# Row 6 subtracted in parts, the last row cut into other pieces, and a first transfer issued by a second engine, in a row-wise sum of |x - y|

## The chip, the cores and the metric

One core of a Trainium2 chip. The metric is device time in microseconds (us). The granted clock is 1.00. The profiled span is some 1.8 us shorter than the time of the same execution (span 86.1 for a time of 87.86), because it leaves out what surrounds the program.

## The reference

```python
def setup_inputs():
    batch, dim = 1024, 4096
    return {"x": np.random.randn(batch, dim).astype(np.float32),
            "y": np.random.randn(batch, dim).astype(np.float32), "axis": -1}

def reference(x, y, axis):
    return np.sum(np.abs(x - y), axis=axis).astype(np.float32)
```

Both inputs are 16.8 MB, so 33.55 MB must come in, and 4 KB go out. With 128 partitions each partition holds 8 rows of 4096 columns, called rows 0 to 7 here.

## The kernel before

VectorE (DVE) subtracts, ScalarE (ACT) takes the absolute value and sums it through its accumulator: each ACTIVATE is followed by an ACTIVATION_READ_ACCUMULATOR that writes the sum out, called the read below. Rows 0 to 3 of x and of y come in one transfer each. Rows 4 to 6 of x come next; their y rows go into the buffer that the first four y rows leave, one transfer as each is used up. Row 7 comes in four pieces, x and y each. The last of the pieces is subtracted and then summed by DVE itself, together with ACT's sums of the others.

```python
PIECES = [2304, 1152, 512, 128]
# ... (K = 8 rows a partition, H = 4, n_part = 3; tiles xa, xb, yb: [128, H, 4096], ro: [128, K])
        nc.sync.dma_start(out=xa, in_=xr[:, 0:H, :])
        nc.sync.dma_start(out=yb, in_=yr[:, 0:H, :])
        nc.sync.dma_start(out=xb[:, 0:H - 1, :], in_=xr[:, H:K - 1, :])

        def whole(tx, ty, k):
            nc.vector.tensor_sub(out=tx, in0=tx, in1=ty)
            nc.scalar.activation(tx, tx, ABS, accum_out=ro[:, k:k + 1])
# ... (rows 0 to 3: whole(); after each, y's row 4, 5, 6 or row 7's x and y pieces are issued)
        for k in range(H - 1):
            whole(xb[:, k, :], yb[:, k, :], H + k)
        tx, ty = xb[:, H - 1, :], yb[:, H - 1, :]
        o = 0
        for i, w in enumerate(PIECES):
            s = slice(o, o + w)
            if i < n_part:
                nc.vector.tensor_sub(out=tx[:, s], in0=tx[:, s], in1=ty[:, s])
                nc.scalar.activation(tx[:, s], tx[:, s], ABS, accum_out=last[:, i:i + 1])
            else:
                nc.vector.tensor_sub(out=last[:, n_part:n_part + w], in0=tx[:, s], in1=ty[:, s])
                nc.vector.reduce_sum(out=ro[:, K - 1:K], in_=last, axis=AX, apply_absolute_value=True)
            o += w
        nc.sync.dma_start(out=orr, in_=ro)
```

Of the kernel before, what the change touches and what calls it, by code (L numbers as in the profile page):

```python
# [5 lines left out]

F32 = mybir.dt.float32
ABS = mybir.ActivationFunctionType.Abs
AX = mybir.AxisListType.X

PIECES = [2304, 1152, 512, 128]


@with_exitstack
def kernel(ctx, tc, x, y, axis, out):
    nc = tc.nc
    P = nc.NUM_PARTITIONS
    R, C = x.shape
    K = R // P
    xr = x.rearrange("(p k) c -> p k c", p=P, k=K)  # L20
    yr = y.rearrange("(p k) c -> p k c", p=P, k=K)
    orr = out.rearrange("(p k) -> p k", p=P, k=K)
    assert sum(PIECES) == C
    n_part = len(PIECES) - 1
    H = K // 2
    ps = ctx.enter_context(tc.tile_pool(name="ps", bufs=1))
    with tc.manual_schedule():
        xa = ps.tile([P, H, C], F32, tag="xa")
        xb = ps.tile([P, H, C], F32, tag="xb")

        yb = ps.tile([P, H, C], F32, tag="yb")
        ro = ps.tile([P, K], F32, tag="ro")

        last = ps.tile([P, n_part + PIECES[-1]], F32, tag="last")
        nc.sync.dma_start(out=xa, in_=xr[:, 0:H, :])  # L35
        nc.sync.dma_start(out=yb, in_=yr[:, 0:H, :])
        nc.sync.dma_start(out=xb[:, 0:H - 1, :], in_=xr[:, H:K - 1, :])

        def whole(tx, ty, k):
            nc.vector.tensor_sub(out=tx, in0=tx, in1=ty)  # L40
            nc.scalar.activation(tx, tx, ABS, accum_out=ro[:, k:k + 1])  # L41

        for k in range(H):
            whole(xa[:, k, :], yb[:, k, :], k)
            if k < H - 1:
                nc.sync.dma_start(out=yb[:, k, :], in_=yr[:, H + k, :])
                continue
            o = 0
            for w in PIECES:
                nc.sync.dma_start(out=xb[:, k, o:o + w], in_=xr[:, K - 1, o:o + w])  # L50
                nc.sync.dma_start(out=yb[:, k, o:o + w], in_=yr[:, K - 1, o:o + w])
                o += w
        for k in range(H - 1):
            whole(xb[:, k, :], yb[:, k, :], H + k)
        tx, ty = xb[:, H - 1, :], yb[:, H - 1, :]
        o = 0
        for i, w in enumerate(PIECES):
            s = slice(o, o + w)
            if i < n_part:
                nc.vector.tensor_sub(out=tx[:, s], in0=tx[:, s], in1=ty[:, s])  # L60
                nc.scalar.activation(tx[:, s], tx[:, s], ABS, accum_out=last[:, i:i + 1])  # L61
# [7 lines that stand above are left out]
# [1 line left out]
_INS = ['x', 'y', 'axis']  # L70
_OUTS = [((1024,), 'float32')]

_NUMBERS = {'axis': -1}


# [26 lines left out]
```

## Time and profile before

| | before |
|---|---|
| time, median of 4 runs | 87.82 us (87.72 to 87.96) |
| profiled span | 86.1 us |
| data coming in | from about 1.7 to 81.4 us, without a rest |
| last reduce ends | 83.77 us |

The busy row of the page (engine, busy us, share of the span, instructions) and the DMA queue (packets, MB, share of 16 engines' span):

```profile
DVE 35.8 (42%) x12; ACT 31.2 (36%) x21; POOL 0.2 (0%) x4
...
q1 hardware_dynamic: 2160, 33.56, 92.0%
```

Neither engine is half busy, while the one DMA queue works for 92% of the span. This is how to read such a kernel: first the stream that carries the data, and its end; then what is left to do after the last byte.

### The profile page before, as it was taken

The page shows a single profiled execution, that of the slowest core. Times are in us where ns is not written, and L with a number is a line of the kernel's source. Part 1 is how long each engine was busy: PE and PEld are TensorE (multiplying, and loading weights), DVE is VectorE, ACT ScalarE, POOL GpSimd, SP SyncE. Part 2 cuts the span into 40 slices and gives each one's busy share as a digit, 9 for nine tenths or more (in the row PEclk, how much of TensorE's full clock was granted, in tenths as well). Part 3 has the DMA queues.
Part 4 walks back from the last instruction along what each step waited for, and adds up shares of the span by engine and source line. Part 5 has one row for each costly group of instructions (what it writes and reads, how often), then busy time and mean ns, then how long its engine had stood idle before and what let it go on. Part 6 is the DMA issues. An engine that isn't in the chain of part 4 may idle for free.

```text
span 86.1 us, 104 instructions
## 1 busy us (share of the span) xinstructions
DVE 35.8 (42%) x12; ACT 31.2 (36%) x21; POOL 0.2 (0%) x4
## 2 busy tenths in 40 slices
DVE  0000000000000000000499999996498989939920
ACT  0000000000410000000004979797933949589970
POOL 0000000000000000000000000000000000000000
DMA  9199999768999999777998889899999999999400
GB/s 426 61 487 487 487 487 487 335 274 365 487 487 487 487 487 487 335 305 335 502 594 365 365 365 457 365 434 442 411 449 411 442 402 411 428 398 401 152 0 2
DMA packets 2160, 33.56 MB, mean 390 GB/s; under 512 B 368, under 2 KB 624, under 8 KB 1136
## 3 DMA queue, kind: packets, MB, share of 16 engines
q1 hardware_dynamic: 2160, 33.56, 92.0%
HBM read 33.55 MB, written 0.00 MB: 390 GB/s over the span
## 4 chain that ended last, share of the span: by engine, by line
DMA 67%; DVE 24%; ACT 5%; SPq 0%; issue 0%; ACTq 0%; DVEq 0%
DMA yb<-in_y_dram 67%; DVE xa L40 20%; ACT xb L61 5%; DVE xb L60 3%; SPq L35 0%; DVE ro L64 0%; ACTq L97 0%; DVEq L60 0%; DVEq L40 0%
## 5 line engine op out<-in xcount | busy, mean ns | idle before, releaser
L40 DVE TENSOR_TENSOR xa<-xa,yb 128x4096 f32<-128x4096 f32 x4 | 17.4, 4420 | 42.0 <-DMA yb<-in_y_dram 42.0
L41 ACT ACTIVATE xa<-xa 128x4096 f32<-128x4096 f32 x4 | 14.5, 3616 | 24.4 <-DVE xa L40 24.4
L40 DVE TENSOR_TENSOR xb<-xb,yb 128x4096 f32<-128x4096 f32 x3 | 13.3, 4426 | 2.9 <-DMA yb<-in_y_dram 2.9
L41 ACT ACTIVATE xb<-xb 128x4096 f32<-128x4096 f32 x3 | 10.8, 3616 | 5.0 <-DVE xb L40 5.0
L41 ACT ACT_TABLE_LOAD x1 | 1.3, 1283 | 22.6 <-DMA xa<-in_x_dram 22.6
L60 DVE TENSOR_TENSOR xb<-xb,yb 128x2304 f32<-128x2304 f32 (+2 forms) x3 | 4.6, 1537 | 1.6 <-DMA yb<-in_y_dram 1.6
L61 ACT ACTIVATE xb<-xb 128x2304 f32<-128x2304 f32 (+2 forms) x3 | 3.9, 1294 | 0.1
L64 DVE TENSOR_REDUCE ro<-last 128x1 f32<-128x131 f32 x1 | 0.3, 290 | 1.5 <-ACT xb L61 1.5
L41 ACT ACTIVATION_READ_ACCUMULATOR xa<-xa 128x1 f32 x4 | 0.7, 186 | 0.0
L41 ACT ACTIVATION_READ_ACCUMULATOR xb<-xb 128x1 f32 x3 | 0.6, 186 | 0.0
L61 ACT ACTIVATION_READ_ACCUMULATOR xb<-xb 128x1 f32 x3 | 0.6, 186 | 0.0
L63 DVE TENSOR_TENSOR last<-xb,yb 128x128 f32<-128x128 f32 x1 | 0.3, 285 | 0.0
L83 POOL MEMSET const-bfloat16-1.0<- 128x1 bf16 x1 | 0.1, 102 | 0.0
L83 POOL MEMSET const-uint8-127<- 128x1 uint8 x1 | 0.1, 101 | 0.0
L83 POOL MEMSET const-float32-0.0<- 128x1 f32 x1 | 0.1, 99 | 0.2 <-issue 0.2
L83 POOL MEMSET const-float32-1.0<- 128x1 f32 x1 | 0.1, 98 | 0.0
## 6 DMA issues: line engine op xcount, KB each, us to landing
xb<-in_x_dram SPq DMA_DIRECT2D x1, 6144.0 KB, 54.8
yb<-in_y_dram SPq DMA_DIRECT2D x3, 2048.0 KB, 15.4
xb<-in_x_dram SPq DMA_DIRECT2D x1, 1152.0 KB, 18.5
yb<-in_y_dram SPq DMA_DIRECT2D x1, 1152.0 KB, 17.3
xb<-in_x_dram SPq DMA_DIRECT2D x1, 576.0 KB, 18.4
yb<-in_y_dram SPq DMA_DIRECT2D x1, 576.0 KB, 19.3
xb<-in_x_dram SPq DMA_DIRECT2D x1, 256.0 KB, 19.5
yb<-in_y_dram SPq DMA_DIRECT2D x1, 256.0 KB, 19.7
```

What stands on the lines that cost most here:

```text
L40: nc.vector.tensor_sub(out=tx, in0=tx, in1=ty)
L41: nc.scalar.activation(tx, tx, ABS, accum_out=ro[:, k:k + 1])
L60: nc.vector.tensor_sub(out=tx[:, s], in0=tx[:, s], in1=ty[:, s])
L61: nc.scalar.activation(tx[:, s], tx[:, s], ABS, accum_out=last[:, i:i + 1])
L63: nc.vector.tensor_sub(out=last[:, n_part:n_part + w], in0=tx[:, s], in1=ty[:, s])
L64: nc.vector.reduce_sum(out=ro[:, K - 1:K], in_=last, axis=AX, apply_absolute_value=True)
L83: nc = _bacc.Bacc("TRN2", target_bir_lowering=False, num_devices=1)
```

## The change

It cuts row 6 into three subtractions and three ACTIVATEs so that ACT may begin before the whole row is subtracted. It makes row 7's pieces more even. It lets ACT issue the first y transfer while SP (SyncE) issues the first x transfer.

```diff
-PIECES = [2304, 1152, 512, 128]
+PIECES = [1984, 1088, 640, 384]
+ROW6 = [2048, 1024, 1024]
@@
+        part6 = ps.tile([P, n6], F32, tag="part6")
@@
-        nc.sync.dma_start(out=yb, in_=yr[:, 0:H, :])
+        nc.scalar.dma_start(out=yb, in_=yr[:, 0:H, :])
@@
-        for k in range(H - 1):
+        for k in range(H - 2):
             whole(xb[:, k, :], yb[:, k, :], H + k)
+        o = 0
+        for i, w in enumerate(ROW6):
+            tx, ty = xb[:, H - 2, o:o + w], yb[:, H - 2, o:o + w]
+            nc.vector.tensor_sub(out=tx, in0=tx, in1=ty)
+            nc.scalar.activation(tx, tx, ABS, accum_out=part6[:, i:i + 1])
+            o += w
@@ in the loop over PIECES
+            if i == 1:
+                nc.vector.reduce_sum(out=ro[:, K - 2:K - 1], in_=part6, axis=AX)
```

More of the change, by code (lines that the diff above doesn't have):

```diff
@@ L24 @@
     n_part = len(PIECES) - 1
+    n6 = len(ROW6)
     H = K // 2
```

## The prediction

> **What bounds the kernel now**
>
> The page's DMA rows and the stretches come first, because 33.55 MB must come in and the engines are busy only 42% and 36% of the span. In the stretches, columns are from:to, length, busy time of each engine, clock, DMA busy share and GB/s:
>
> ```profile
> 4.30:15.00 10.70, 0.00 (x0) 0.00 (x0) 0.00 (x0) 1.00 1.13 490
> ...
> 60.00:76.80 16.80, 13.28 (x3) 11.78 (x7) 0.00 (x0) 1.00 1.00 422
> ```
>
> A share above 1 is an artefact: a packet counts where it starts. What is to be seen is that the DMA engines do not rest from the first packet to the last. The list of DMA issues, with the time from issue to landing, gives the landings:
>
> ```profile
> xb<-in_x_dram SPq DMA_DIRECT2D x1, 1152.0 KB, 18.5
> yb<-in_y_dram SPq DMA_DIRECT2D x1, 1152.0 KB, 17.3
> xb<-in_x_dram SPq DMA_DIRECT2D x1, 576.0 KB, 18.4
> yb<-in_y_dram SPq DMA_DIRECT2D x1, 576.0 KB, 19.3
> xb<-in_x_dram SPq DMA_DIRECT2D x1, 256.0 KB, 19.5
> yb<-in_y_dram SPq DMA_DIRECT2D x1, 256.0 KB, 19.7
> ...
> yb<-in_y_dram SPq DMA_DIRECT2D x1, 64.0 KB, 10.3
> xa<-in_x_dram SPq DMA_DIRECT2D x1, 21.8
> yb<-in_y_dram SPq DMA_DIRECT2D x1, 40.7
> ```
>
> Issue times from the timeline (0.73 for xa, 1.16 for the first y, then 55.49, 59.45, 59.82, 60.30, 60.79, 61.35 and 71.14) plus these give: xa lands at 22.5, the first y at 41.9, x2304 at 74.0, y2304 at 76.8, x1152 at 78.2, y1152 at 79.6, x512 at 80.3, y512 at 81.05, y128 at 81.4. Between xa and the first y, 8.39 MB came in 19.4 us: 433 GB/s. Every late transfer waits 10 to 19 us in the queue, so the data stream sets its own pace; nothing the engines do delays it.
>
> So the span is a data stream that ends at 81.4, and a tail from there to 86.1. The timeline (start, duration, engine, operation, idle time before) shows the tail:
>
> ```profile
> 70.71 3.62 ACT L41 ACTIVATE xb<-xb 128x4096 f32<-128x4096 f32 x1 [1.11 <-DVE xb L40]
> 71.14 0.33 SPq L51 DMA_DIRECT2D yb<-in_y_dram  x1
> 71.15 4.43 DVE L40 TENSOR_TENSOR xb<-xb,yb 128x4096 f32<-128x4096 f32 x1 [0.47 <-DMA yb<-in_y_dram]
> 74.23 0.19 ACT L41 ACTIVATION_READ_ACCUMULATOR xb<-xb 128x1 f32 x1
> 75.61 3.62 ACT L41 ACTIVATE xb<-xb 128x4096 f32<-128x4096 f32 x1 [1.19 <-DVE xb L40]
> 76.88 2.56 DVE L60 TENSOR_TENSOR xb<-xb,yb 128x2304 f32<-128x2304 f32 x1 [1.30 <-DMA yb<-in_y_dram]
> 79.13 0.19 ACT L41 ACTIVATION_READ_ACCUMULATOR xb<-xb 128x1 f32 x1
> 79.47 2.12 ACT L61 ACTIVATE xb<-xb 128x2304 f32<-128x2304 f32 x1
> ...
> 81.59 1.15 ACT L61 ACTIVATE xb<-xb 128x1152 f32<-128x1152 f32 x1
> 81.74 0.28 DVE L63 TENSOR_TENSOR last<-xb,yb 128x128 f32<-128x128 f32 x1
> ...
> 82.74 0.61 ACT L61 ACTIVATE xb<-xb 128x512 f32<-128x512 f32 x1
> 83.26 0.18 ACT L61 ACTIVATION_READ_ACCUMULATOR xb<-xb 128x1 f32 x1
> 83.48 0.29 DVE L64 TENSOR_REDUCE ro<-last 128x1 f32<-128x131 f32 x1 [1.45 <-ACT xb L61]
> ```
>
> The last subtraction is over at 82.0, yet the reduce waits 1.45 us for ACT. ACT runs three pieces without a gap from 79.47: that tail hangs on the 2304 piece's subtraction (ends 79.45), and ACT was not free earlier either (row 6 ended at 79.32). The tail after the last landing is 83.77 - 81.4 = 2.4 us of work, then 2.3 us from the reduce's end to the span's end for the store.
>
> **What the Trainium skill says**
>
> "DMA: Bandwidth & Descriptors", section "Issuing engines are not separate DMA queues": issuing on several engines at once saves only the sequencer's issue time. The trace agrees as far as it can: an issue takes 0.38 to 0.43 us while data queues for 20 us and more. The same page, "Queues, rings and completion order": SP and ACT own one ring each on the same 16 engines, which serve rings in turn. The trace before has one queue only, so this is untested.
>
> "VectorE: DVE Perf Modes", section on the TRN2 errata: fp32 tensor_tensor takes (N+151)/0.96 ns. The trace agrees: 693 ns at 512 columns, 2558 at 2304. Its tier table has tensor_reduce at one element per cycle too: 131 columns took 290 ns. "ScalarE: Activation LUTs", "What ACT_TABLE_LOAD costs": an ACTIVATE with immediates takes 186 + 0.833 N ns. The trace has 612 ns at 512 and 1146 at 1152, as stated, and 2123 at 2304, 17 ns more.
>
> **The change part by part**
>
> *First y transfer on ACT.* Removes 0.43 us of issue from SP, adds one issue to an idle ACT. Both streams share 433 GB/s, so xa and the first y should both land near 41.9, where only the later one was needed before. The first subtraction starts at 41.99 plus whatever lead the third transfer (xb) takes in the queue. The slack for a late start is the 2.00 us that DVE idles before row 4 (61.43). ACT's table load now waits for a later landing (41.9 instead of 22.6), but 41.9 + 1.28 is before the first ACTIVATE at 46.45. Worth 0.0 us.
>
> *The stream's end.* Landing intervals in the tail: 2304 columns 2.8 us, 1152 1.43, 512 0.7; about 0.09 + 1.18 us per 1000 columns. From row 6's landing (71.12, just before DVE's 71.15), the new pieces 1984, 1088, 640 and 384 take 2.43, 1.37, 0.845 and 0.54 us each for x and for y. y1984 lands at 75.98, y1088 at 78.73, y640 at 80.42, y384 at 81.50. The end is 0.1 us later than now, for more even pieces.
>
> *Row 6 in parts.* DVE: 2291, 1224 and 1224 ns, less some 0.09 us of overlap at each joint as rows 0 to 3 show (4 x 4.42 done in 17.43): 71.15 to 73.44, 74.58, 75.72. That is 0.13 us more than now and ends before the next landing. ACT could start at 73.47 instead of 75.61, but row 5's accumulator read holds it until 74.32. Its pieces last 1.91, 1.04 and 1.04 us: 76.23, 77.27, 78.31. One row costs 0.37 us more on ACT, but ends 78.3 plus the read instead of 79.3: 1.0 us earlier.
>
> *Row 7.* Sub of 1984, 2.22 us from 75.98 + 0.10: ends 78.30. ACT takes it at 78.33, 1.85 us, to 80.18. The new 3-column reduce waits for row 6's last accumulator (78.4), costs about 0.16 us (estimate: the 290 ns of 131 columns less 128 cycles at 1.04 ns), and is over at 78.6, before y1088 lands. Sub of 1088: 78.83 to 80.12; ACT 80.18 to 81.28 (1.09). Sub of 640: 80.52 to 81.35; ACT (0.72) 81.38 to 82.10, accumulator read to 82.19. Sub of 384: 81.60 to 82.16. The reduce of 387 columns (0.16 + 384 x 1.04 ns = 0.56 us) starts at 82.22 and ends at 82.78. Against 83.77 that is 0.99 us less. Sum: head 0.0, DVE's row 6 hidden, tail -1.0 us. 87.85 - 1.0 = 86.9 us.
>
> **The rivals**
>
> 1. *The two queues are not fair, and y lands late.* If xb gets ahead of the first y by some of its 48 KB rows (6.29 MB in 128 rows), DVE starts late. For it: xb is behind xa on the queue that SP starts. Against it: both transfers are equal in size and issued within half a microsecond. Up to 2 us late costs nothing (the idle before row 4); 3.6 us late puts row 6's subtraction about 1 us late and ACT's chain with it, which eats the gain: 87.7.
> 2. *Two streams move less, or more, than one.* Each per cent over the first 40 us is 0.4 us, and the stream's end carries straight to the end. More is unlikely: 433 GB/s hardly varies now. The start has 21.8 us for xa from issue, of which 19.4 are data; if parallel issue trims the 2.4 us of start-up by 0.4, the result is 86.5. Lost rate makes it 87.3.
> 3. *DVE becomes the bound at the end.* The last 384 columns need 0.1 + 0.56 + 0.56 us after landing: 82.72, only 0.06 below the ACT path. If the small reduce is held by ACT until after 78.7 it pushes the 1088 subtraction and all after it; ACT has 0.3 us of room there. This would make 87.2.
> 4. *The uneven split was already hidden.* If row 6 on ACT stays the bound (it does if row 5 runs late), the gain halves: 87.4.
>
> **Range and chances**
>
> The tail's durations are all measured in this trace, good to 0.1 us each, and three paths (ACT, DVE, data) end within 0.1 us of each other, so misses add lateness rather than gain. The queues' sharing is what the trace cannot show: a few tenths either way. The runs of before spread over 0.24 us. So 86.9, from 86.2 to 87.7. Over 2% faster means below 86.1: it needs a gain in the head as well; 0.09. Slower by 2% means an unfair queue: 0.03.
>
> **What would show it**
>
> The first subtraction starts at 42 to 44 and xa lands near 41 instead of 22.5; two queues stand in the DMA rows with the same total. DVE still idles before row 4. ACT's first row 6 part starts near 74.3, its last ends near 78.3; the 1984 ACTIVATE starts within 0.1 us of its subtraction's end; the last reduce starts near 82.2 after a short wait, its input 387 columns. The last y landing near 81.5 shows the stream untouched; an end before 81 would show a gain in the head that I do not expect. A first subtraction after 44, a wait of more than 0.3 us of the small reduce, or a last landing after 82 would prove it wrong.

## The result, and the profile after

| | before | after |
|---|---|---|
| median of 4 runs | 87.82 us (87.72 to 87.96) | 86.80 us (86.68 to 87.36) |
| ratio | | 0.9894 (95%: 0.9855 to 0.9932) |

A ratio is the mean time of one kernel's runs over that of the other's in the same rounds, so it is not quite the ratio of the two medians. The gain is 1.0 us, 1.1%: clear of the noise, since the interval leaves out 1.

The profile taken with this result fell on the slowest of the four executions (87.36 us, span 85.6). Its DMA view has both queues, and the issues with their time to landing:

```profile
q1 hardware_dynamic: 2016, 25.17, 70.4%
q10 hardware_dynamic: 144, 8.39, 22.7%
...
yb<-in_y_dram ACTq DMA_DIRECT2D x1, 41.6
xa<-in_x_dram SPq DMA_DIRECT2D x1, 41.4
```

The queue that ACT feeds moved the 8.39 MB of the first y. With both issued at 0.73, xa and the first y now land together, at 42.1 and 42.3, where xa had landed at 22.5 before.

The kernel was profiled once more, unaltered, and that profile (86.73 us, span 84.9) shows its usual execution. Its timeline (start, us, engine, line, operation, idle before; x3 stands for three instructions in a row, here the three parts of row 6):

```profile
71.08 4.56 DVE L61 TENSOR_TENSOR xb<-xb,yb 128x2048 f32<-128x2048 f32 x3 [0.46 <-DMA yb<-in_y_dram]
...
74.26 1.89 ACT L62 ACTIVATE xb<-xb 128x2048 f32<-128x2048 f32 x1
75.97 2.23 DVE L71 TENSOR_TENSOR xb<-xb,yb 128x1984 f32<-128x1984 f32 x1 [0.33 <-DMA yb<-in_y_dram]
...
78.14 0.19 ACT L62 ACTIVATION_READ_ACCUMULATOR xb<-xb 128x1 f32 x1
78.24 1.85 ACT L72 ACTIVATE xb<-xb 128x1984 f32<-128x1984 f32 x1
78.36 0.16 DVE L69 TENSOR_REDUCE ro<-part 128x1 f32<-128x3 f32 x1 [0.16 <-ACT xb L62]
78.70 1.29 DVE L71 TENSOR_TENSOR xb<-xb,yb 128x1088 f32<-128x1088 f32 x1 [0.19 <-DMA yb<-in_y_dram]
...
80.09 1.09 ACT L72 ACTIVATE xb<-xb 128x1088 f32<-128x1088 f32 x1
...
81.21 0.74 ACT L72 ACTIVATE xb<-xb 128x640 f32<-128x640 f32 x1
81.35 0.56 DVE L74 TENSOR_TENSOR last<-xb,yb 128x384 f32<-128x384 f32 x1 [0.17 <-DMA yb<-in_y_dram]
...
82.07 0.56 DVE L75 TENSOR_REDUCE ro<-last 128x1 f32<-128x387 f32 x1 [0.17 <-ACT xb L72]
```

Three things are to be seen. ACT starts row 6 at 74.26, while DVE is still subtracting that row, and the 1984 ACTIVATE starts at 78.24 instead of the 79.47 of the 2304 one. The 1984 subtraction ends at 78.20 and row 6's last accumulator read begins at 78.14, 0.10 before ACT takes the next piece: both conditions are met within 0.1 us of each other. And the last reduce waits 0.17 us for ACT, not 1.45.

How early the stream brings row 6's y differs between executions, so in what follows I use a length that leaves this out: from the start of row 6's first subtraction to the end of the last reduce. Before it was 83.77 - 71.15 = 12.62 us. Afterwards it is 82.63 - 71.08 = 11.55 in the usual execution, and 11.56 in the slow one of the first profile, whose row 6 started at 71.72. The 0.6 us between those two executions is thus a late data stream, and not the tail.

### The profile page after: what moved, and what is told of

It reads as the page before. It is cut to its first block, busy times and chain, and to the rows that moved or that the text cites. A ratio compares the mean times of both kernels' runs of the same rounds, so it can differ in the third digit from the quotient of the medians.

```text
span 85.6 us, 111 instructions
## 1 busy us (share of the span) xinstructions
DVE 36.5 (43%) x15; ACT 31.2 (36%) x25; POOL 0.2 (0%) x4
## 3 DMA queue, kind: packets, MB, share of 16 engines
q10 hardware_dynamic: 144, 8.39, 22.7%
## 4 chain that ended last, share of the span: by engine, by line
DMA 67%; DVE 16%; ACT 13%; issue 0%; ACTq 0%
DMA yb<-in_y_dram 67%; DVE xa L43 10%; DVE xb L43 5%; ACT xb L62 5%; ACT xb L44 4%; ACT xb L72 4%; DVE ro L75 1%; ACTq L108 0%
## 5 line engine op out<-in xcount | busy, mean ns | idle before, releaser
L43 DVE TENSOR_TENSOR xa<-xa,yb 128x4096 f32<-128x4096 f32 x4 | 17.4, 4420 | 42.3 <-DMA yb<-in_y_dram 42.3
L43 DVE TENSOR_TENSOR xb<-xb,yb 128x4096 f32<-128x4096 f32 x2 | 8.8, 4425 | 2.6 <-DMA yb<-in_y_dram 2.6
L44 ACT ACTIVATE xb<-xb 128x4096 f32<-128x4096 f32 x2 | 7.2, 3617 | 4.1 <-DVE xb L43 4.1
L61 DVE TENSOR_TENSOR xb<-xb,yb 128x1024 f32<-128x1024 f32 (+1 forms) x3 | 4.6, 1576 | 0.5 <-DMA yb<-in_y_dram 0.5
L71 DVE TENSOR_TENSOR xb<-xb,yb 128x1984 f32<-128x1984 f32 (+2 forms) x3 | 4.3, 1448 | 0.9 <-DMA yb<-in_y_dram 0.9
L62 ACT ACTIVATE xb<-xb 128x1024 f32<-128x1024 f32 (+1 forms) x3 | 4.0, 1324 | 0.0
L72 ACT ACTIVATE xb<-xb 128x1984 f32<-128x1984 f32 (+2 forms) x3 | 3.7, 1229 | 0.0
L75 DVE TENSOR_REDUCE ro<-last 128x1 f32<-128x387 f32 x1 | 0.6, 556 | 0.2 <-ACT xb L72 0.2
L74 DVE TENSOR_TENSOR last<-xb,yb 128x384 f32<-128x384 f32 x1 | 0.6, 559 | 0.1
```

What stands on the lines that cost most here:

```text
L62: nc.scalar.activation(tx, tx, ABS, accum_out=part6[:, i:i + 1])
```

## The experiments

All ten runs gave correct results. "Tail" is the length just defined, read from each run's profile. The kernel before was timed beside each batch: 87.80 in the first, 87.79 in the second, 88.09 in the third, with single runs up to 88.79 in the first. The batches ran on three chips, and such late runs of the kernel before raise its mean, so in the first two batches the ratios are 0.1 to 0.3% lower than those of the medians.

| run | median us | ratio to before (95%) | tail us |
|---|---|---|---|
| kernel before | 87.82 | | 12.62 |
| first y on ACT alone | 87.79 | 0.9976 (0.9938 to 1.0014) | 12.54 |
| row 6 in parts alone | 87.90 | 0.9984 (0.9945 to 1.0024) | 12.55 |
| new pieces alone | 87.75 | 0.9974 (0.9933 to 1.0015) | 12.41 |
| row 6 and pieces, all from SP | 86.91 | 0.9874 (0.9828 to 0.9920) | 11.61 |
| changed kernel again | 86.82 | 0.9878 (0.9841 to 0.9915) | 11.55 |
| changed, last pieces 896, 128 | 87.58 | 0.9966 (0.9930 to 1.0002) | 12.42 |
| changed, row 6 in two parts | 86.79 | 0.9870 (0.9836 to 0.9903) | 11.53 |
| row 6 and pieces, first y 2 us late | 86.84 | 0.9876 (0.9842 to 0.9910) | 11.56 |
| row 6 and pieces, first y 5 us late | 88.93 | 1.0103 (1.0069 to 1.0137) | 12.03 (see there) |
| changed, row 5 in parts too | 86.76 | 0.9851 (0.9819 to 0.9884) | 11.56 |

My theory was that of the prediction: the stream sets its own end, and the gain comes when ACT may start row 7 earlier. That needs two things at once: ACT through with row 6, and the first piece subtracted. The rival was that the parts of the change add up.

The tail repeats to 0.01 us where the code is the same (11.55 and 11.56), but it contains the stream that brings row 7, and that scatters by about 0.1 us. The profile of the kernel before had a long one, so 12.54 and 12.55 in the table mean no gain, and the gain of the whole change is 1.0 us rather than the 1.07 between 12.62 and 11.55.

**The first y transfer on ACT, alone**

```diff
-        nc.sync.dma_start(out=yb, in_=yr[:, 0:H, :])
+        nc.scalar.dma_start(out=yb, in_=yr[:, 0:H, :])
```

> The kernel before with the first y transfer issued by ACT and nothing else. My theory: the two queues only share the same stream, so the time stays at 87.8 us within 0.2; xa and the first y both land near 42, the first subtraction starts at 42.0 to 42.5, DVE still idles 1.5 to 2.2 us before row 4. Rival: two queues make the stream itself slower or less even, then the last y lands up to 0.5 us later than 81.4 and the time is 88.0 to 88.3. Second rival: issuing side by side trims the start, then the time is 87.4.

The median is 87.79 us, the first subtraction started at 42.03, and the tail is what it was within that scatter. The interval includes 1. So this part brings nothing that five rounds can tell.

**Row 6 in parts, alone**

```diff
 PIECES = [2304, 1152, 512, 128]
+ROW6 = [2048, 1024, 1024]     # and the loop and the small reduce of the change
```

> The kernel before with row 6 in three parts and nothing else (old pieces 2304, 1152, 512, 128, all transfers from SP). My theory: ACT is through with row 6 near 78.4 instead of 79.3, but the 2304 piece's subtraction still ends at 79.45, so ACT waits about 1.0 us for it and the end does not move: 87.8 us within 0.1. Rival: the three parts of the change add up, and this part brings some 0.5 us alone: 87.3.

From its timeline, ACT's last accumulator read of row 6 and its first piece of row 7:

```profile
78.56 0.18 ACT L62 ACTIVATION_READ_ACCUMULATOR xb<-xb 128x1 f32 x1
...
79.77 2.12 ACT L72 ACTIVATE xb<-xb 128x2304 f32<-128x2304 f32 x1 [1.02 <-DVE xb L71]
```

ACT was free 1.02 us early and waited exactly that long for the subtraction of the 2304 piece. The time did not fall. The rival, a gain of some 0.5 us of its own, is out. (This profile fell on a late execution, 88.16 us, whose row 6 started 0.36 us later than in the kernel before.)

**The new pieces, alone**

```diff
-PIECES = [2304, 1152, 512, 128]
+PIECES = [1984, 1088, 640, 384]
```

> The kernel before with pieces 1984, 1088, 640, 384 and nothing else. My theory: the 1984 subtraction ends at 78.3, but ACT is in row 6 until 79.32; then 1.85 + 1.09 + 0.72 us to 82.98, the read to 83.07, and a reduce of 0.56 us from 83.11 to 83.67, against 83.77 before: 0.1 us less, 87.7 us. Rival: the parts add up and this one brings about 0.5 us alone: 87.3.

```profile
76.11 2.23 DVE L60 TENSOR_TENSOR xb<-xb,yb 128x1984 f32<-128x1984 f32 x1 [0.48 <-DMA yb<-in_y_dram]
...
79.28 1.84 ACT L61 ACTIVATE xb<-xb 128x1984 f32<-128x1984 f32 x1
...
83.05 0.56 DVE L64 TENSOR_REDUCE ro<-last 128x1 f32<-128x387 f32 x1 [1.04 <-ACT xb L61]
```

Now the subtraction is done at 78.34, and ACT cannot take it before 79.28, without any idle time before it: ACT was still in row 6. The last reduce waits 1.04 us. This is the mirror image of the run before, and again the time stays: 87.75 against 87.80. The interval of the ratio reaches down to 0.9933, which would be 0.6 us, so it does not rule out the rival's 0.5 us; the tail does. It is 0.13 to 0.14 us shorter than in the two runs above, where 0.1 was expected.

**Both together, all transfers from SP**

```diff
-        nc.scalar.dma_start(out=yb, in_=yr[:, 0:H, :])
+        nc.sync.dma_start(out=yb, in_=yr[:, 0:H, :])     # in the changed kernel
```

> Row 6 in parts and the new pieces together, but all transfers from SP as before. My theory: the whole gain is here, 1.0 us: 86.8 us, the last reduce from 82.2 to 82.8, and the 1984 ACTIVATE starts within 0.1 us of both its subtraction's end and the end of row 6 on ACT. Rival: the transfer issued by ACT brings part of the gain, then this is 87.1 to 87.4.

```profile
76.19 2.23 DVE L71 TENSOR_TENSOR xb<-xb,yb 128x1984 f32<-128x1984 f32 x1 [0.42 <-DMA yb<-in_y_dram]
...
78.30 0.19 ACT L62 ACTIVATION_READ_ACCUMULATOR xb<-xb 128x1 f32 x1
78.45 1.86 ACT L72 ACTIVATE xb<-xb 128x1984 f32<-128x1984 f32 x1
...
82.26 0.56 DVE L75 TENSOR_REDUCE ro<-last 128x1 f32<-128x387 f32 x1 [0.17 <-ACT xb L72]
```

The subtraction ends at 78.42 and ACT takes the piece at 78.45, just after its last read of row 6. The median is 86.91 us. Two edits of which one alone is worth nothing and the other 0.1 us are worth 1.0 us together (the tail fell to 11.61), and the transfer on ACT has no share in it: the ratio is 0.9874 without it and 0.9878 with it, in the next run.

**The changed kernel again**

No edit.

> The changed kernel once more, unaltered, because the profile on record fell on its slowest execution (87.36 us, span 85.6, against 84.9 to 85.1 of the others). My theory: the late 0.5 us of that execution lies in the data stream alone (row 6's y landed at 71.69 instead of 71.1), not in the change; median 86.8 us, and in a profile with a span near 85.0 row 6's y lands near 71.1 and the last reduce starts near 82.2. Rival: two queues often bring a late stream; then half of the runs or more are near 87.3.

All six runs lie between 86.73 and 87.02. A late execution is not a mark of two queues either: the kernel with all transfers from SP had one of 87.38, and the kernel before, all from SP too, has several above 88.2. What makes a stream late in some executions was not looked into and stays open.

**The last piece small again**

```diff
-PIECES = [1984, 1088, 640, 384]
+PIECES = [1984, 1088, 896, 128]
```

> The changed kernel with pieces 1984, 1088, 896, 128 instead of 1984, 1088, 640, 384: 256 columns go back from the last piece, which only DVE handles, to the third, which ACT handles. My theory: y896 lands at 81.0, DVE subtracts to 82.2, ACT (0.93 us) ends at 83.2, the reduce of 131 columns runs from 83.3 to 83.6: 87.6 us, so most of the gain hangs on the last piece's size. Rival: the first piece's earlier landing is what counts and the last piece does not matter: 86.8 us.

```profile
82.18 0.95 ACT L72 ACTIVATE xb<-xb 128x896 f32<-128x896 f32 x1 [0.85 <-DVE xb L71]
...
83.26 0.29 DVE L75 TENSOR_REDUCE ro<-last 128x1 f32<-128x131 f32 x1 [0.91 <-ACT xb L72]
```

Row 6 in parts and the 1984 piece are both there, yet the median is 87.58. The third piece landed late because it is large, ACT idled 0.85 us for it, and the reduce then idled 0.91 us for ACT. So the gain needs a third condition: enough of the last columns must stay with DVE, which would otherwise only wait.

**Row 6 in two parts**

```diff
-ROW6 = [2048, 1024, 1024]
+ROW6 = [2048, 2048]
```

> The changed kernel with row 6 in two parts of 2048 columns instead of three. My theory: ACT would be through with row 6 some 0.2 us earlier (78.1 instead of 78.3), but the 1984 piece's subtraction ends at 78.3 all the same, so 86.8 us within 0.15: two parts are enough. Rival: finer parts matter for ACT's start: then 0.3 us slower or more, 87.1.

The median is 86.79: two parts do as well as three. Row 6 started at 71.21 in this execution, 0.13 us later than in the repeated profile. Counted from there, ACT began its last read of row 6 0.20 us earlier (78.07 - 71.21 = 6.86 instead of 7.06), as expected, but it then waited for the 1984 subtraction and took the piece after 7.14 instead of 7.16 us.

**The first y 2 us late, and 5 us late**

Both have row 6 in parts and the new pieces, with everything issued by SP in this order (the edit is shown against the run with all transfers from SP):

```diff
+        xbf = xb.rearrange("p k c -> p (k c)")
+        xrf = x.rearrange("(p k) c -> p (k c)", p=P, k=K)
+        E = 1664                       # 4096 in the other run
+        nc.sync.dma_start(out=xbf[:, 0:E], in_=xrf[:, H * C:H * C + E])
         nc.sync.dma_start(out=yb, in_=yr[:, 0:H, :])
-        nc.sync.dma_start(out=xb[:, 0:H - 1, :], in_=xr[:, H:K - 1, :])
+        nc.sync.dma_start(out=xbf[:, E:(H - 1) * C], in_=xrf[:, H * C + E:(K - 1) * C])
```

> Row 6 in parts and the new pieces, all transfers from SP, with the first 1664 columns of row 4's x brought in before the first y, so that the first y lands about 2.0 us late (43.9) while the stream as a whole is the same. My theory (rival 1 of the prediction): DVE's 2.0 us of idle time before row 4 goes to nearly 0 and the end does not move: 86.9 us within 0.2. Rival: every us of a later first subtraction is lost: 88.9 us.

> As the run with the first y 2 us late, but with all of row 4's x (4096 columns) before the first y, which then lands about 4.9 us late (46.8). My theory: beyond the 2.0 us of slack the lateness comes through: rows 0 to 3 end at 64.3, row 6's last subtraction at 77.6, ACT is through with row 6 near 80.8 and the last reduce ends near 85.1 instead of 82.8: 89.2 us, and DVE has no idle time before row 4. Rival: the stream alone sets the end whatever DVE's start: 86.9. Second rival: all 4.9 us are lost: 91.8.

With 2 us, the timeline shows rows 0 to 3 and then row 4:

```profile
44.21 17.43 DVE L47 TENSOR_TENSOR xa<-xa,yb 128x4096 f32<-128x4096 f32 x4 [44.21 <-DMA yb<-in_y_dram]
...
61.71 4.42 DVE L47 TENSOR_TENSOR xb<-xb,yb 128x4096 f32<-128x4096 f32 x1
```

The first subtraction is 2.2 us later than before, no idle time is left ahead of row 4, and the median is 86.84: the slack took it all. With 5 us it did not:

```profile
46.84 17.43 DVE L47 TENSOR_TENSOR xa<-xa,yb 128x4096 f32<-128x4096 f32 x4 [46.84 <-DMA yb<-in_y_dram]
...
80.56 1.84 ACT L76 ACTIVATE xb<-xb 128x1984 f32<-128x1984 f32 x1
80.68 0.16 DVE L73 TENSOR_REDUCE ro<-part 128x1 f32<-128x3 f32 x1 [1.14 <-ACT xb L66]
...
84.33 0.56 DVE L79 TENSOR_REDUCE ro<-last 128x1 f32<-128x387 f32 x1 [1.07 <-ACT xb L76]
```

The last reduce ended at 84.89 (85.1 was expected) and the median is 88.93 (89.2 expected), 2.0 us above the all-SP kernel for 4.9 us of lateness (by the ratios too: 1.0103 - 0.9874 of 87.8 us). I had left out the 0.09 us by which a subtraction overlaps the one that it follows at once. Why 4.9 us cost 2.0 and not 2.9: before row 4 the kernel before idles 2.00 us, but it idles another 0.40 and 0.47 us before rows 5 and 6, and these took their part too. Row 6 started at 72.86, 1.71 us later than in the kernel before, and the tail is 12.03 us, because ACT now runs late from row 5 on. The small reduce also waits 1.14 us for ACT and holds up the 1088 subtraction behind it; this costs nothing here, since the last reduce still waits 1.07 us for ACT.

**Row 5 in parts as well**

```diff
-        for k in range(H - 2):
+        for k in range(H - 3):
             whole(xb[:, k, :], yb[:, k, :], H + k)
+        parts(H - 3, part5)            # the loop of row 6, for row 5
+        parts(H - 2, part6)
@@ in the loop over PIECES
+            if i == 0:
+                nc.vector.reduce_sum(out=ro[:, K - 3:K - 2], in_=part5, axis=AX)
```

> The changed kernel with row 5 in three parts too, which frees ACT of row 6 near 77.6 instead of 78.3. My theory: the end does not move, because the 1984 piece's subtraction ends at 78.3 whatever ACT does; ACT now idles some 0.7 us before the 1984 ACTIVATE: 86.8 us within 0.15. Rival: ACT's chain from row 5 on is the bound, as the chain of waits of the changed kernel has it: 86.1.

```profile
77.99 0.18 ACT L65 ACTIVATION_READ_ACCUMULATOR xb<-xb 128x1 f32 x1
...
78.93 1.86 ACT L80 ACTIVATE xb<-xb 128x1984 f32<-128x1984 f32 x1 [0.76 <-DVE xb L79]
```

ACT idles 0.76 us where it had none, and the tail is 11.56, as without this edit. (The profile fell on a late execution, 87.41 us.) The chain of waits of the changed kernel runs through ACT without a gap from row 5 to the last reduce, which suggests that ACT alone is the bound. This run shows that it is not. Freeing ACT only hands the wait to the first piece's subtraction, that is, to the stream that brings it.

No run beats the changed kernel by more than the spread of its own runs. The one with two parts does the same with less.

## Why the prediction was right

**Point and range.** 86.9 was predicted and 86.80 measured, inside 86.2 to 87.7. None of the three signs of being wrong appeared: even in the late first profile the first subtraction started at 42.33, the small reduce waited 0.16 us and the last y landed at 81.9.

**The stream.** Right: it went on without a rest, and the two queues shared it. The 0.1 us that I added "for more even pieces" is no effect of the pieces. The formula behind it, 0.09 us for a transfer and 1.18 us for 1000 columns, gives 10.39 us for the old pieces as well as for the new ones, because both cut the same 4096 columns of x and of y into eight transfers. From the landing of row 6's y to that of the last y the trace of the kernel before has 10.27 us, so 0.1 us is what the formula misses there. The other profiles show no effect either: 10.17 and 10.13 us in the two other runs with the old pieces, 10.16 to 10.28 in the eight with the new ones. In the repeated profile it was 10.20, 0.18 us less than the predicted 81.50 - 71.12 = 10.38. About 0.1 us of that came through, by way of the 640 piece: its ACTIVATE had to wait for its subtraction and began 81.21 - 71.08 = 10.13 us after row 6's start, against 81.38 - 71.15 = 10.23 in the working.

**First y on ACT, worth 0.0.** Right, shown by that part alone and by leaving it out of the rest. The slack of 2.00 us for a late first y was right too: 2.2 us late cost nothing, 4.9 us late cost 2.0. Its loss for a y that is 3.6 us late, 87.7 - 86.9 = 0.8 us, was not tried, but it fits an estimate from the last run: 2.0 us less the 1.3 us between 4.9 and 3.6.

**Row 6 on ACT, 1.0 us earlier.** Right in its times, 0.1 us too much in its difference. The predicted start at 74.32 and end at 78.31 are 74.26 and 78.24 in the repeated profile, whose row 6 started 0.07 us earlier. The 2048 ACTIVATE took 1.893 us, not 1.91. But the "1.0 us earlier" compares the end of the last ACTIVATE, 78.31, with 79.32, which is the end of the read after it. ACTIVATE against ACTIVATE, row 6 ended 75.61 + 3.62 - 71.15 = 8.08 us after its start before and 78.24 - 71.08 = 7.16 afterwards: 0.92 us earlier. The sum is not touched by this slip, because row 7 was worked out from 78.31 itself.

**Row 7, 0.99 us less.** The tail was worked out as 82.78 - 71.15 = 11.63 and measured as 11.55: 1.07 us less than in the profile before, and 1.0 less than in the two other runs with the old pieces (12.54 and 12.55). The order of events was as told, down to the tie between ACT and the first subtraction. The rival "DVE becomes the bound" gave DVE only 0.06 us of room; with the earlier stream it was 0.17.

**What the prediction did not say.** It added the parts in a chain of times, which carried the interaction without naming it. Its rival 4, a bound that stays with row 6 on ACT, was treated as a way to lose half. The single-part runs show that it loses nearly all: the tail stays at 12.41 us with the pieces alone and at 12.55 with row 6 alone, against 11.55 with both.

## What to carry to other kernels

Where an instruction waits for two things that come at nearly the same time, removing either wait alone gains next to nothing (here 0.0 and 0.1 us, against 1.0 for both); before dismissing an edit that measured as zero, see from the trace which second condition stood just behind it, and move both. When one engine runs without a gap to the end, that is not yet proof that it is the bound: give it slack, and look whether it then idles. The transfer issued from a second queue brought nothing here (87.79 against 87.80 us), where one queue already kept the DMA engines busy for 92% of the span.

## What the Trainium skill lacked or had wrong

- "ScalarE: Activation LUTs", "What ACT_TABLE_LOAD costs": its 186 + 0.833 N ns holds for an ACTIVATE that follows another at once (640 columns: 719 ns in the run with the pieces alone), but one that had to wait for DVE took 17 to 18 ns more (640 columns: 737 ns in the repeated profile; 1984 columns: 1840 in the run with the pieces alone, 1857 in the one with row 6 in two parts). The prediction had seen the 17 ns at 2304 columns without this reason. The page names the accumulator output and gives it no cost, and no other page gives the read's: each accumulating ACTIVATE has a read of 186 ns after it. Because the read overlaps on both sides by some 0.09 us, three parts of row 6 start 1.90 and 1.04 us apart (74.26, 76.16, 77.20), which is their own durations and no more.
- "DMA: Bandwidth & Descriptors", "Queues, rings and completion order": it says that rings are served in turn by packets, and gives a packet's size in descriptors but not in bytes. Here a turn was a whole 64 KB partition row on each of the 16 engines. From 33.0 to 35.8 us of the repeated profile the 16 packets that started, 1.05 MB in all, were of ACT's queue, and from 35.8 to 38.0 of SP's; from 1.7 to 39 us the two queues alternate in this way, eight turns each (a packet counts where it starts, hence the share above 100%):

```profile
q10 hardware_dynamic: 16, 1.05, 86.4%
...
q1 hardware_dynamic: 16, 1.05, 109.9%
```

- The same page, "Measured (HBM→SBUF, 128 partitions, SWDGE, issued from GpSimd)", advises transfers of 1 MiB and more. Queued behind others, transfers of 192 KB (384 columns) did better than that may lead one to expect: in the repeated profile they landed 0.52 and 0.47 us after the one before, 377 and 416 GB/s. Yet cutting is not free. The eight transfers of row 7 (4.19 MB) took 10.20 us, 411 GB/s, while row 6's y before them, one transfer of 2.10 MB, took 4.89 us, 429 GB/s. At that rate row 7 would have taken 9.78 us, so by this estimate the cuts cost some 0.4 us.
